# Gated embedding added to the residual by accumulating transfers instead of VectorE, in three of four column groups

## The chip, the core and the metric

The kernel runs on one core of one Trainium2 chip. The metric is the device time of one execution in microseconds (us), taken as the median over several runs of the same program. The profile is one further execution, recorded by the hardware profiler.

Five instruction streams matter here. TensorE (PE) multiplies matrices into the banks of PSUM. VectorE (DVE) and ScalarE (ACT) work on tiles of 128 rows. GpSimd (POOL) does almost no arithmetic in this kernel, but the transfers that add into their destination are issued from it. SyncE (SP) issues all the plain loads and stores of the part in question. Each engine takes its own instructions in a fixed order, and an instruction that waits for another engine or for a transfer holds back everything that stands behind it on its engine.

## The reference, cut to what matters

The block computes a residual stream `h` of 256 rows by 4096 columns (attention heads and a convolution module in parallel, projected and added to the input). The last stage, which the change touches, is this:

```python
gate = jax.nn.sigmoid(rms_norm(h, ple_norm_g[i]) @ w_ple_gate[i] + b_ple_gate[i])
h = h + gate * (p[i] @ w_ple[i])
return rms_norm(h, final_g)
```

`w_ple_gate` is 4096 x 4096 and `w_ple` is 256 x 4096, all in float32. The final norm needs, for each row, the sum of the squares of the new `h` over all 4096 columns before any column can be scaled and stored.

## The kernel before

**Products.** Every matrix product is done on high and low parts of its operands: ACT rounds a weight tile to a short format (`wh`, line 204), DVE subtracts that from the tile (`wl`, line 205), and PE adds three products (high by high, low by high, high by low). `mixed_product` computes a pair of 512-column blocks (1024 columns) for both halves of 128 rows. It walks over 16 pairs of weight row blocks. Half of the pairs in the last stage are done with seven block products instead of eight (a form of Strassen's method, marked `*` in the order strings): for these DVE also makes sums of weights (`ua`, `ub`, lines 518, 519, 531, 532), ACT and DVE split these sums (`uh`, `ul`), and four more PSUM banks, `P1`, `P5`, `P6` and `P7`, collect the helper products. The eight PSUM banks are thus used up: four hold the main sums `acc`, and four (the pool `ps_tmp`) hold the helpers. A plain pair is 24 matmuls, a pair of seven is 21.

**The last stage.** `gated_pair` (from line 1236 on) does one group of 1024 columns; it is called for three groups (`c0` = 0, 2, 4, here called G1, G2, G3), and the fourth group, G4, is written out behind it. At a group's end the product `p @ w_ple` of its columns is put into the four `ps_tmp` banks as `pacc`. Then four quarters follow (two blocks of columns by two halves of rows): DVE finishes the gate's argument (line 1266), ACT takes the sigmoid (line 1267), and four things are left for later: the multiplication of the gate with `pacc` (`z<-acc,z`, which I call the multiply), the addition to the residual (`hc<-hc,z`, the add), the sum of squares on ACT (line 610, the square), and the multiplication with the final norm's weight (`hc<-hc,row`, the weighting).

**What sets the order.** The deque `later` holds the work that is left over. `fill(4)` takes four entries from it after each pair of the next group, and so mixes the left work with the splitting of the next group's weights. The first pair of G2, G3 and G4 is plain (pair 1), the second is one of seven (pair `0*`), so the four `ps_tmp` banks must have been emptied by the multiplies before that second pair's helper products can begin. A scheduler then orders all instructions of each engine by their place in the program and by when it expects their inputs; only what is pinned keeps its place. Work therefore moves on all engines where the entries of `later` change.

Of the kernel before, what the change touches and what calls it, by code (L numbers as in the profile page):

```python
# [13 lines left out]
ALU = mybir.AluOpType  # L14
# [11 lines left out]
def hybrid_block(  # L26
# [23 lines left out]
    nc = tc.nc  # L50
# [129 lines left out]
    later = deque()  # L180
# [62 lines left out]
    def product(w, col, lhs, kblocks, pool=None, tag="acc", fills=2):  # L243

        acc = [
            (pool or ps_acc).tile([P, NB], F32, tag=tag, name=f"acc{h}") for h in range(NH)
        ]
        for k0 in range(0, kblocks, KC):
            kc = min(KC, kblocks - k0)
            wh, wl = weight_parts(w, col, k0, kc)  # L250
            for k in range(kc):
                for h in range(NH):
                    accumulate(acc[h], h, lhs, k0 + k, wh, wl, k, kblocks)
            fill(fills)
        return acc
# [313 lines left out]
    tt, stt = nc.vector.tensor_tensor, nc.vector.scalar_tensor_tensor  # L569
    QUARTERS = ((0, 0), (1, 0), (0, 1), (1, 1))  # L570

    def helper_sums(helper, z):


        nc.scalar.copy(z[1][0], helper["P1"])
        tt(z[1][0], helper["P6"], z[1][0], ALU.add)
        tt(z[0][1], helper["P5"], z[1][0], ALU.add)
        tt(z[1][0], helper["P7"], z[1][0], ALU.add)
        tt(z[1][1], helper["P5"], z[1][0], ALU.add)

    def sum_tiles(*homes):

        homes = homes or (dict(tag="stage"),) * 2
        t = [spool.tile([P, NH, NB], F32, name="z", **kw) for kw in homes]
        return t, [[t[j][:, h] for j in range(2)] for h in range(NH)]
# [481 lines left out]
    def broadcast_row(src, n0, n, **kw):  # L1067

        kw = kw or dict(tag="row", bufs=3)
        t = spool.tile([P, n], F32, name="row", **kw)  # L1070
        nc.sync.dma_start(
            t, bass.AP(tensor=src.tensor, offset=src.offset + n0, ap=[[0, P], [1, n]])
        )
        return t
# [122 lines left out]
    for c0 in range(0, D // NB, 2):  # L1197
        for j in range(2):
            hc = act.tile([P, NH, NB], F32, tag="act", name="hc")
# [20 lines left out]
        for h, j in QUARTERS:  # L1220
            hc = hs[c0 + j][:, h, :]
# [10 lines left out]
    ssq_f = cpool.tile([P, NH, n_f + 2], F32, name="ssq_f")  # L1232
    nc.vector.memset(ssq_f[:, :, :1], EPS)
    square_f = partial(square_sum, scale=D ** -0.5)

    def gated_pair(c0, order, ahead):

        z, rows, fgs = [], [], []

        def on_begin():  # L1240
            rows.extend(broadcast_row(b_ple_gate, (c0 + j) * NB, NB) for j in range(2))

        def on_helpers(helper):
            z.extend(sum_tiles()[1])
            stt(z[0][0], helper["P1"], r_h[:, :1], rows[0], ALU.mult, ALU.add)
            helper_sums(helper, z)
            for h, j in QUARTERS[1:]:
                zz = z[h][j]
                stt(
                    zz, zz, r_h[:, h : h + 1], rows[j],  # L1250
                    ALU.mult, ALU.subtract if j else ALU.add,
                )
            fgs.extend(broadcast_row(final_g, (c0 + j) * NB, NB) for j in range(2))

        acc = mixed_product(
            w_ple_gate[0], c0 * NB, hT, hS, order, on_helpers, ahead=ahead, fills=(4,),
            on_begin=on_begin,
        )
        pacc = [
            product(w_ple[0], (c0 + j) * NB, pT, PLE // P, pool=ps_tmp, tag="tmp", fills=0)  # L1260
            for j in range(2)
        ]
        todo = []
        for h, j in QUARTERS:
            gt, hc = z[h][j], hs[c0 + j][:, h, :]
            stt(gt, acc[h][j], r_h[:, h : h + 1], gt, ALU.mult, ALU.subtract if j else ALU.add)
            nc.scalar.activation(gt, gt, AF.Sigmoid)
            later.append(partial(tt, gt, pacc[j][h], gt, ALU.mult))
            todo.append(partial(tt, hc, hc, gt, ALU.add))
            todo.append(partial(square_f, ssq_f[:, h, 1 + c0 + j : 2 + c0 + j], hc))  # L1270
            todo.append(partial(tt, hc, hc, fgs[j], ALU.mult))
        later.extend(todo)

    for c0 in range(0, n_f - 2, 2):
        gated_pair(c0, dense if c0 else late, None if c0 else h_ahead)


    c0 = n_f - 2
# [9 lines left out]
    rows, fgs = [], []  # L1288
# [90 lines left out]
    squares = []  # L1379
# [45 lines left out]
```

## Time and profile before

| quantity | value |
|---|---|
| median of 3 runs | 2024.87 us |
| the 3 runs | 2024.87, 2024.77, 4118.48 us |
| profiled execution, device time | 2025.85 us |
| its span in the profile | 2024.1 us |
| mean granted PE clock | 0.998 |
| PE busy | 2006.7 us (99%) |
| DVE busy | 1926.9 us (95%) |
| ACT busy | 1257.1 us (62%) |
| POOL busy | 65.3 us (3%) |
| POOL transfers in the last stage | none (last one issued at 1615.2 us) |

The one run of 4118.48 us is twice the others and says nothing on the kernel; the other two agree. The profiled execution's own time stands 1.75 us above its span and 0.98 us above the median. In the trace's time, G1 ends and G2 begins at about 1745.6 us, G3 begins at 1833.3 us, G4 at 1921.2 us, and the span ends at 2024.1 us. "Busy" means that an instruction was being executed; waiting for a semaphore is not busy time.

### The profile page before, as it was taken

What the parts mean: (1) busy time and instruction counts of PE and PEld (TensorE: products, weight loads), DVE (VectorE), ACT (ScalarE), POOL (GpSimd) and SP (SyncE); (2) the same over time, 40 slices, a digit from 0 to 9 for tenths busy, and PEclk for the clock granted to TensorE, in tenths of its full rate; (3) what the DMA queues carried; (4) which work ended last, traced back from release to release, by engine and by line L of the source; (5) the groups of instructions that cost most, each with busy time, mean ns of one, the idle gap of its engine ahead of it and who ended that gap; (6) DMA issues with size and microseconds to landing.
All of it is one profiled execution on the core that took longest, in us unless ns stands there. A gap on an engine that the chain in (4) does not pass through costs nothing.

```text
span 2024.1 us, 26329 instructions
## 1 busy us (share of the span) xinstructions
PE 2006.7 (99%) x9043; PEld 1648.0 (81%) x9043; DVE 1926.9 (95%) x2771; ACT 1257.1 (62%) x1634; POOL 65.3 (3%) x71
## 2 busy tenths in 40 slices
PE   9999999999999999999999999999999999999997
PEld 7888888878888888788888888887888888888876
DVE  7999999899999999888999999999999999999998
ACT  7655555665666556776566676765766766656565
POOL 0000000000000000000000000000000000000000
PEclk9999999999999999999999999999999999999999
DMA  8788878679668877556677786876767766666765
GB/s 290 225 233 241 249 221 250 178 220 257 200 198 257 255 206 235 164 176 205 202 239 215 225 244 209 240 239 204 236 215 230 234 200 200 211 218 206 232 207 180
DMA packets 174193, 447.72 MB, mean 221 GB/s; under 512 B 14302, under 2 KB 17518, under 8 KB 174058
## 3 DMA queue, kind: packets, MB, share of 16 engines
q1 hardware_dynamic: 161952, 417.93, 63.8%
q0 software_dynamic: 11456, 27.27, 7.9%
q8 instruction: 71, 1.16, 0.2%
q10 hardware_dynamic: 650, 0.84, 0.1%
q14 instruction: 64, 0.52, 0.1%
HBM read 441.78 MB, written 4.19 MB: 220 GB/s over the span
## 4 chain that ended last, share of the span: by engine, by line
PE 89%; DVE 6%; issue 2%; DMA 1%; ACT 1%; POOLq 0%; POOL 0%; ACTq 0%; DVEq 0%; SPq 0%
PE acc L420 68%; PE acc_P L420 17%; DVE wl L205 2%; DMA wt<-in_w_in_dram 1%; PE tmp_ps L170 1%; DVE cv L787 1%; PE acc L237 1%; DVE ul L205 1%; PE tmp_ps L959 0%; PE tmp_ps L943 0%; PE tmp_ps L977 0%; ACT uh L204 0%; DVE cv L868 0%; ACT wh L204 0%; PE tmp_ps L982 0%
## 5 line engine op out<-in xcount | busy, mean ns | idle before, releaser
L420 PE MATMUL acc<-wh,big_t 128*128 128x512 f32 x4028 | 1240.3, 391 | 0.9 <-ACT big_t L156 0.4
L204 ACT CAST wh<-wt 128x1024 fp32r<-128x1024 f32 (+1 forms) x716 | 684.3, 965 | 493.8 <-PE acc L420 351.7
L420 PEld LDWEIGHTS acc<-wh,big_t 128*128 128x128 f32 x4028 | 753.3, 188 | 157.1 <-issue 1.3
L205 DVE TENSOR_TENSOR wl<-wt,wh 128x1024 fp32r<-128x1024 f32 (+1 forms) x716 | 788.8, 1113 | 33.0 <-ACT wh L204 27.5
L420 PE MATMUL acc<-wl,big_t 128*128 128x512 f32 x1958 | 756.4, 392 | 0.3 <-DVE wl L205 0.2
L420 PEld LDWEIGHTS acc<-wl,big_t 128*128 128x128 f32 x1958 | 367.2, 188 | 78.1 <-DVE wl L205 2.7
L204 ACT CAST uh<-ua 128x1024 fp32r<-128x1024 f32 x187 | 196.6, 1051 | 103.0 <-DVE ua L519 51.7
L205 DVE TENSOR_TENSOR ul<-ua,uh 128x1024 fp32r<-128x1024 f32 x187 | 228.1, 1220 | 6.9 <-ACT uh L204 4.2
L787 DVE SCALAR_TENSOR_TENSOR cv<-uT,dw,cv 128x255 f32<-128x255 f32 (+23 forms) x480 | 203.6, 463 | 1.1
L420 PE MATMUL acc_P<-uh,big_t 128*128 128x512 f32 x570 | 174.6, 391 | 0.1
L204 ACT CAST uh<-ub 128x1024 fp32r<-128x1024 f32 x99 | 104.2, 1053 | 47.9 <-DVE ub L532 39.2
L420 PEld LDWEIGHTS acc_P<-uh,big_t 128*128 128x128 f32 x570 | 106.0, 188 | 24.5 <-ACT uh L204 3.3
L205 DVE TENSOR_TENSOR ul<-ub,uh 128x1024 fp32r<-128x1024 f32 x99 | 120.8, 1220 | 0.8 <-ACT uh L204 0.5
L420 PE MATMUL acc_P<-ul,big_t 128*128 128x512 f32 x285 | 109.7, 392 | 0.2 <-DVE ul L205 0.2
L420 PE MATMUL acc<-uh,big_t 128*128 128x512 f32 x286 | 88.6, 390 | 0.0
L420 PE MATMUL acc_P<-wh,big_t 128*128 128x512 f32 x286 | 88.3, 389 | 0.0
L518 DVE TENSOR_TENSOR ua<-wt 128x512 f32<-128x512 f32 x112 | 76.9, 686 | 10.0 <-DMA wt<-in_w_in_dram 6.2
L519 DVE TENSOR_TENSOR ua<-wt 128x512 f32<-128x512 f32 x112 | 76.8, 686 | 2.7 <-DMA wt<-in_w_in_dram 1.7
L420 PE MATMUL acc_P<-uh,comb_t 128*128 128x512 f32 x228 | 70.3, 391 | 0.3 <-ACT uh L204 0.2
L532 DVE TENSOR_TENSOR ub<-ub,wt 128x512 f32<-128x512 f32 x99 | 68.1, 688 | 1.4
L531 DVE TENSOR_TENSOR ub<-ua,wt 128x512 f32<-128x512 f32 x99 | 67.8, 685 | 0.0
L420 PEld LDWEIGHTS acc_P<-ul,big_t 128*128 128x128 f32 x285 | 53.3, 188 | 13.9 <-DVE ul L205 3.0
(254 smaller groups left out, 1631.0 us busy)
## 6 DMA issues: line engine op xcount, KB each, us to landing
wt<-in_w_in_dram SPq DMA_DIRECT2D x416, 512.0 KB, 4.7
wt<-in_w_out_dram SPq DMA_DIRECT2D x128, 512.0 KB, 4.5
wt<-in_w_ple_gate_dram SPq DMA_DIRECT2D x128, 512.0 KB, 4.2
wt<-in_w_pw_dram SPq DMA_DIRECT2D x32, 512.0 KB, 4.9
ua<-in_w_in_dram SPq DMA_DIRECT2D x31, 512.0 KB, 4.3
ua<-in_w_in_dram POOLq DMA_DIRECT2D x31, 512.0 KB, 8.8
wt<-in_w_in_dram SPq DMA_DIRECT2D x31, 256.0 KB, 2.8
low<-in_w_in_dram POOLq DMA_DIRECT2D x12, 512.0 KB, 8.2
```

What stands on the lines that cost most here:

```text
L170: nc.tensor.transpose(pt[:, i * T + h * P : i * T + (h + 1) * P], src[:, h, b] if len(src.shape) == 4 else src[:, h, b * P : (b + 1) * P], ...
L204: nc.scalar.copy(wh[:, :kc, :], wt[:, :kc, :]),
L205: nc.vector.tensor_tensor(wl[:, :kc, :], wt[:, :kc, :], wh[:, :kc, :].bitcast(F32), ALU.subtract),
L237: nc.tensor.matmul(acc, a, b[:, k, :], start=kb == 0 and kind == 0, stop=kb == kblocks - 1 and kind == 2,)
L420: nc.tensor.matmul(banks[name], a, b, start=name not in begun, stop=final and ends[name] == n and kind == 2 and not (left and name in "P2 ...
L518: plus(ua[:, 0], w0[:, 0], w0[:, 1])
L519: plus(ua[:, 1], w0[:, 1], w1[:, 1])
L531: plus(ub[:, 0], ua[:, 0], w1[:, 1])
L532: plus(ub[:, 1], ub[:, 0], w1[:, 0])
L787: nc.vector.scalar_tensor_tensor(cv[:, i, PAD - k :], uT[:, i, : T + k - PAD], dw[:, b, k : k + 1], cv[:, i, PAD - k :], ALU.mult, ALU.add,)
```

## The change

Two edits in `gated_pair`, so in the three groups G1 to G3; G4 is as it was.

```diff
-        todo = []
+        squares, weights = [], []
         for h, j in QUARTERS:
             gt, hc = z[h][j], hs[c0 + j][:, h, :]
             stt(gt, acc[h][j], r_h[:, h : h + 1], gt, ALU.mult, ALU.subtract if j else ALU.add)
             nc.scalar.activation(gt, gt, AF.Sigmoid)
             later.append(partial(tt, gt, pacc[j][h], gt, ALU.mult))
-            todo.append(partial(tt, hc, hc, gt, ALU.add))
-            todo.append(partial(square_f, ssq_f[:, h, 1 + c0 + j : 2 + c0 + j], hc))
-            todo.append(partial(tt, hc, hc, fgs[j], ALU.mult))
-        later.extend(todo)
+            later.append(partial(nc.gpsimd.dma_start, hc, gt, accum_op=ALU.add))
+            squares.append(partial(square_f, ssq_f[:, h, 1 + c0 + j : 2 + c0 + j], hc))
+            weights.append(partial(tt, hc, hc, fgs[j], ALU.mult))
+        later.extend(squares + weights)
```

The add of each quarter, a DVE instruction on 128 x 512 float32, becomes a transfer issued from POOL that reads `gt` in SBUF and adds it into `hc` in SBUF: 256 KB each, 12 in all. The 16 entries of a group also stand in another sequence. Before: four multiplies, then add, square, weighting of each quarter. Now: multiply and transfer of each quarter in turn, then four squares, then four weightings. With four entries taken after each pair, two multiplies and two transfers are now taken behind the first pair, the other two of each behind the second (`0*`), the squares behind the third and the weightings behind the fourth.

The scheduler makes of this the following. First ACT at the start of G2, with the sigmoids of G1 behind us. `uh_15712`, `wh_15716` and `uh_15723` are the high parts for pair `0*`; `hc_11728` and `hc_11730` are the residual blocks of G1, `junk` the unused output of a square. A semaphore whose name begins with `DMASW` belongs to a transfer issued from POOL. Before:

```order
L204 CAST wh_15677<-wt_15659 128x1024 [waits DMAHW0_49,PE_49,Activation_49]
L204 CAST wh_15705<-wt_15697 128x512 [waits DMAHW1_49,PE_49,Activation_49]
L204 CAST uh_15712<-ua_15709 128x1024 [waits DVE_49]
L204 CAST wh_15716<-wt_15699 128x1024 [waits DMAHW4_49,PE_49,Activation_49]
L204 CAST wh_15761<-wt_15757 128x1024 [waits DMAHW5_49,DVE_49,PE_49]
L204 CAST wh_15777<-wt_15759 128x1024 [waits DMAHW6_49,DVE_49,PE_49]
L204 CAST uh_15723<-ub_15720 128x1024 [waits DVE_49]
L610 ACTIVATE junk_15753,ssq_f_14773<-hc_11728 128x512
L204 CAST wh_15803<-wt_15799 128x512 [waits DMAHW7_49,PE_49,Activation_49]
L610 ACTIVATE junk_15793,ssq_f_14773<-hc_11728 128x512 [waits DVE_49,Activation_49]
```

And ACT at the same place now:

```order
L204 CAST uh_15712<-ua_15709 128x1024 [waits DVE_49]
L610 ACTIVATE junk_15792,ssq_f_14773<-hc_11728 128x512 [waits DMASW4_49]
L610 ACTIVATE junk_15794,ssq_f_14773<-hc_11728 128x512 [waits DMASW5_49,Activation_49]
L204 CAST wh_15716<-wt_15699 128x1024 [waits DMAHW4_49,PE_49]
L204 CAST uh_15723<-ub_15720 128x1024 [waits DVE_49]
L204 CAST wh_15760<-wt_15756 128x1024 [waits DMAHW5_49,PE_49]
L204 CAST wh_15776<-wt_15758 128x1024 [waits DMAHW6_49,PE_49]
L610 ACTIVATE junk_15796,ssq_f_14773<-hc_11730 128x512 [waits DMASW6_49,Activation_49]
L204 CAST wh_15804<-wt_15800 128x512 [waits DMAHW7_49,DVE_49,PE_49]
L610 ACTIVATE junk_15798,ssq_f_14773<-hc_11730 128x512 [waits DMASW7_49,Activation_49]
L204 CAST uh_15811<-ua_15808 128x1024 [waits DVE_49]
```

All four squares moved up, each in front of a cast for the next matmuls, and each now waits for a transfer. At the starts of G3 and G4 ACT's order is nearly the same, except that one square, not two, stands ahead of the cast that corresponds to `wh_15716`.

Then DVE at the same place. `z_15518` and `z_15519` hold the gates, `acc1_15606`, `acc0_15625` and `acc1_15626` are banks with `pacc`. Before:

```order
L184 TENSOR_TENSOR z_15518<-acc1_15606,z_15518 128x512 [waits PE_49,Activation_49]
L519 TENSOR_TENSOR ua_15709<-wt_15697,wt_15699 128x512 [waits DMAHW4_49]
L184 TENSOR_TENSOR z_15519<-acc0_15625,z_15519 128x512 [waits PE_49,Activation_49]
L205 TENSOR_TENSOR wl_15678<-wt_15659,wh_15677 128x1024 [waits DMAHW0_49,DVE_49,Activation_49]
L184 TENSOR_TENSOR z_15519<-acc1_15626,z_15519 128x512 [waits PE_49]
L205 TENSOR_TENSOR wl_15706<-wt_15697,wh_15705 128x512 [waits DVE_49,Activation_49]
L205 TENSOR_TENSOR ul_15713<-ua_15709,uh_15712 128x1024 [waits Activation_49]
L205 TENSOR_TENSOR wl_15717<-wt_15699,wh_15716 128x1024 [waits PE_49,Activation_49]
L531 TENSOR_TENSOR ub_15720<-ua_15709,wt_15699 128x512
L184 TENSOR_TENSOR hc_11728<-hc_11728,z_15518 128x512
```

And DVE now:

```order
L184 TENSOR_TENSOR z_15518<-acc1_15606,z_15518 128x512 [waits PE_49,Activation_49]
L519 TENSOR_TENSOR ua_15709<-wt_15697,wt_15699 128x512 [waits DMAHW4_49]
L531 TENSOR_TENSOR ub_15720<-ua_15709,wt_15699 128x512 [waits DVE_49]
L205 TENSOR_TENSOR wl_15678<-wt_15659,wh_15677 128x1024 [waits DMAHW0_49,Activation_49]
L205 TENSOR_TENSOR wl_15706<-wt_15697,wh_15705 128x512 [waits DVE_49,PE_49,Activation_49]
L205 TENSOR_TENSOR ul_15713<-ua_15709,uh_15712 128x1024 [waits Activation_49]
L532 TENSOR_TENSOR ub_15720<-ub_15720,wt_15699 128x512 [waits DVE_49]
L205 TENSOR_TENSOR wl_15717<-wt_15699,wh_15716 128x1024 [waits PE_49,Activation_49]
L184 TENSOR_TENSOR z_15519<-acc0_15625,z_15519 128x512
L205 TENSOR_TENSOR ul_15724<-ub_15720,uh_15723 128x1024 [waits Activation_49]
L184 TENSOR_TENSOR z_15519<-acc1_15626,z_15519 128x512
```

The third multiply (of `acc0_15625`) moved behind `wl_15717`, which needs the cast `wh_15716`, and the fourth behind `ul_15724`; the adds are gone. Further on in DVE's order the four weightings now stand close together behind the second pair of seven (`2*`), at the sums `ub_15819` and ahead of `ul_15823`.

Last, PE at the helper products of pair `0*`, as they stand now:

```order
L420 MATMUL acc_P7_15703<-uh_15712,big_t_14665 128x512 [waits DVE_49]
L420 MATMUL acc_P7_15703<-uh_15712,big_t_14665 128x512
L420 MATMUL acc_P7_15703<-ul_15713,big_t_14665 128x512
L420 MATMUL acc00_15653<-wh_15716,big_t_14664 128x512 [waits Activation_49]
L420 MATMUL acc00_15653<-wh_15716,big_t_14664 128x512
L420 MATMUL acc00_15653<-wl_15717,big_t_14664 128x512
```

Before, the first of these rows had no wait of its own; now it waits for DVE, namely for the third multiply to empty the bank that `P7` takes over.

## The prediction

> **What bounds the kernel now.** I read the page first (busy time by engine), then the stretches of the last stage, then the chain of waits in order of time.
>
> ```profile
> span 2024.1 us, 26329 instructions
> PE 2006.7 (99%) x9043; PEld 1648.0 (81%) x9043; DVE 1926.9 (95%) x2771; ACT 1257.1 (62%) x1634; POOL 65.3 (3%) x71
> PE 89%; DVE 6%; issue 2%; DMA 1%; ACT 1%; POOLq 0%; POOL 0%; ACTq 0%; DVEq 0%; SPq 0%
> ```
>
> PE is the bound, with DVE right behind it. For the last stage the next view gives, by stretch, the length, then the busy time of each engine, the clock, and the transfers' share and rate.
>
> ```profile
> core 0: us, PE busy (x) PEld busy (x) DVE busy (x) ACT busy (x) POOL busy (x), PEclk, DMA share, GB/s
> 1746.00:1784.00 38.00, 37.95 (x167) 30.70 (x166) 37.97 (x47) 23.00 (x31) 0.00 (x0) 1.00 0.62 201
> 1784.00:1834.00 50.00, 50.00 (x221) 41.06 (x220) 49.30 (x60) 29.47 (x33) 0.00 (x0) 1.00 0.71 228
> 1834.00:1872.00 38.00, 38.00 (x166) 30.72 (x166) 37.85 (x48) 23.09 (x31) 0.00 (x0) 1.00 0.62 192
> ```
>
> Both engines are full: at each group's start (first and third row) DVE is busy for practically all of it, while ACT has 15 us to spare in 38 and POOL does nothing. How much PE could gain is read from the chain, whose rows give start and length:
>
> ```profile
> 1740.13 5.44 PE acc L237 x24
> ...
> 1827.88 5.44 PE acc L237 x24
> ...
> 1915.73 5.44 PE acc L237 x24
> ```
>
> These are the same 24 matmuls at the ends of G1, G2 and G3. One takes 5.44 / 24 = 0.2267 us of PE's time. A group has 8 x 24 + 8 x 21 + 24 = 384, so 87.05 us, and the groups follow each other after 87.75 and 87.85. PE waits 0.7 and 0.8 us in a group; with about 1 us in G4, 2.5 us is the most that any relief of DVE at these three places can bring.
>
> **The adds leave DVE.**
>
> ```profile
> L184 DVE TENSOR_TENSOR hc<-hc,z 128x512 f32<-128x512 f32 x12 | 8.1, 685 | 0.0
> L610 ACT ACTIVATE junk<-hc 128x512 bf16<-128x512 f32 (+1 forms) x33 | 20.3, 615 | 5.0 <-DVE hc L1332 2.3 <-DVE hc L1222 1.3 <-DVE end L1342 1.0
> ```
>
> Twelve adds of 0.60 us (start to start in the rows below) are 7.2 us of DVE, 2.4 a group. The gain is not 7.2 but at most the 2.5 us above, since PE is the next limit at once. The squares and the weightings keep their number and price; only their places change.
>
> **The transfers' own price.** Twelve issues occupy an idle POOL. The nearest rows: the accumulating loads of 512 KB (issue on POOL, time to landing), the two queues, a plain store of 256 KB out of the same tile, and the plain weight load.
>
> ```profile
> q1 hardware_dynamic: 161952, 417.93, 63.8%
> q0 software_dynamic: 11456, 27.27, 7.9%
> wt<-in_w_ple_gate_dram SPq DMA_DIRECT2D x128, 512.0 KB, 4.2
> out_dram<-hc SPq DMA_DIRECT2D x12, 256.0 KB, 2.4
> ...
> L524 POOL DMA_DIRECT2D low<-in_w_out_dram x6: 859/860/872, 1445.6 to 1615.2; - x6
> ...
> DMA to landing us min/median/max: 5.8/8.3/10.0
> ```
>
> The last row is for all 21 loads of that kind. In q0 all the traffic is accumulating: 0.079 x 2024.1 us for 27.27 MB, so 3.07 us of 16 engines for 512 KB, against 1.62 us in q1. Half the bytes take 1.5 us off the median of 8.3 if a transfer has the engines alone, and 3.1 if it shares them evenly: 6.8 or 5.2 us. Off the fastest, 5.8, it leaves 4.3. I call the time from issue to landing T and take 5.3, close to the lower value, because a source in SBUF rather than memory should be no slower, and these transfers share the engines (share 0.62). The ends: at least 2.4 + 0.87 = 3.3 us (the plain store plus POOL's issue), at most 8.4 (as slow as twice the bytes). The load on the engines, 12 x 1.5 = 18 us in 264, raises a share of about 0.65 by 0.07; I cost it at nothing, since weight loads that land in 4.2 us are issued ahead into five tiles. If that cover is gone, DVE's sums `ua` are late first.
>
> [...]
>
> **What now stands behind the transfers.** This is the term that decides. At the start of G2, DVE, ACT and PE before (start, length):
>
> ```profile
> 1743.34 1.28 DVE L184 TENSOR_TENSOR z<-acc,z 128x512 f32<-128x512 f32 x2
> ...
> 1747.47 0.68 DVE L205 TENSOR_TENSOR wl<-wt,wh 128x512 fp32r<-128x512 f32 x1
> 1748.07 1.22 DVE L205 TENSOR_TENSOR ul<-ua,uh 128x1024 fp32r<-128x1024 f32 x1
> 1749.23 1.23 DVE L205 TENSOR_TENSOR wl<-wt,wh 128x1024 fp32r<-128x1024 f32 x1
> 1750.38 0.69 DVE L531 TENSOR_TENSOR ub<-ua,wt 128x512 f32<-128x512 f32 x1
> ```
>
> ```profile
> 1745.95 1.05 ACT L204 CAST uh<-ua 128x1024 fp32r<-128x1024 f32 x1
> 1748.15 1.06 ACT L204 CAST wh<-wt 128x1024 fp32r<-128x1024 f32 x1 [1.14 <-issue]
> ...
> 1753.68 0.63 ACT L610 ACTIVATE junk<-hc 128x512 bf16<-128x512 f32 x1
> 1754.21 0.19 ACT L610 ACTIVATION_READ_ACCUMULATOR junk<-hc 128x1 f32 x1
> 1754.30 0.61 ACT L204 CAST wh<-wt 128x512 fp32r<-128x512 f32 x1
> ```
>
> ```profile
> 1752.21 0.61 PE L420 MATMUL acc_P<-uh,big_t 128*128 128x512 f32 x2
> ...
> 1766.04 0.39 PE L420 MATMUL acc_P<-ul,big_t 128*128 128x512 f32 x1
> ```
>
> The steps from start to start: DVE 0.60 us for 512 columns and 1.14 to 1.16 for 1024, ACT 0.62 for a square.
>
> - The first multiply ends at 1744.0, so the first transfer lands at 1744.1 + 5.3 = 1749.4, the second, behind POOL's 0.87 us of issue, at about 1750.4. ACT is done with `uh` at 1747.0 and stands before the first square. The second square ends at 1751.1. Only then comes the cast of `wh` that began at 1748.15.
> - Behind it: cast 1.05, subtraction 1.14, third multiply 0.60, plus hand-over: 1754.0. PE wants the bank that this multiply frees at 1752.21: a wait of 1.8 us.
> - The third transfer, issued at 1754.0, lands at 1759.3. Behind it stand, in series, the third square 0.62, a cast of 512 columns 0.56, its `wl` 0.60, three sums 1.8, a weighting 0.60, `ul` 1.14, `wl` 1.14, the last sum 0.60, three weightings 1.8, `wl` 1.14 and `ul` 1.14. That is 11.1 us, so this `ul` is ready at about 1770.6. The fourth transfer's square is ready before this chain needs it.
> - Before, PE took that `ul` at 1766.04, with three more matmuls (0.7 us) already behind it. G2 is late by 4.6 + 0.7 = 5.3 us.
>
> G3 is milder, since one square, not two, stands ahead of the cast, and that cast came late before too:
>
> ```profile
> 1830.79 0.69 DVE L184 TENSOR_TENSOR z<-acc,z 128x512 f32<-128x512 f32 x1
> ...
> 1835.85 1.06 ACT L204 CAST wh<-wt 128x1024 fp32r<-128x1024 f32 x1 [2.05 <-PE acc L420]
> ...
> 1854.31 0.39 PE L420 MATMUL acc_P<-ul,big_t 128*128 128x512 f32 x1
> ```
>
> First multiply done at 1831.4, landing 1836.8, square, cast from 1837.45 (not 1835.85), third multiply done at 1840.3, landing 1845.7, and 11.1 us later 1856.8 instead of 1854.31: 2.5 us, and 0.4 for the order of matmuls, 2.9. G4 has the same order: 2.9.
>
> **The sum.** 5.3 + 2.9 + 2.9 = 11.1 us. Of the 2.5 us that PE waits now, the part that lies further on in the groups, which a lighter DVE ends, I put at 1.5. Net 9.6 us on the profiled execution's 2025.85: 2035.4; that execution stands 1.0 above the median, so 2034.4 against 2024.87. I say 2035, slower by 0.5%. Since two landings stand in series at each of three places, each us of T is worth 6 us: at T = 3.7 the sum is nothing, at 8.4 it is 9.6 + 6 x 3.1 = 28.
>
> **The rivals.**
> - *The transfers are hidden* (chance 0.22). If T is at most 3.7, the squares find their blocks ready, DVE's 2.4 us a group remain as a gain, and PE's waits of 2.5 us go: 2022.4 to 2025. For it speaks the plain store (2.4 us), against it the fastest accumulating load, 5.8.
> - *The transfers are slower, or one waits for the other* (0.22). At T = 8.4 the time is 2053. If the second of a pair starts when the first has landed, the second square of G2 comes 4.3 us later and the chains of G3 and G4 some 2.5: about 2044. For it speaks the slowest load (10.0); nowhere before do two such transfers stand back to back, so the trace excludes neither.
> - *More than 2% slower* (0.03) would need 40 us, so T near 10, or weight loads that come late throughout.
> - The forecast itself, T from 3.7 to 6.5, so 2025 to 2042, has 0.53.
>
> The range from 2022 to 2053 takes in both ends of T (2022.4 and 2053), and so the forecast, the hidden case and most of the slow one; about 1 in 10 is left out. A change of 2%, 40 us, is about what a measurement of this kernel can tell from none. The ceiling of 2.5 us makes faster by that much as good as impossible (0.01), slower 0.03, within 0.96.
>
> **What would show it.** Right: squares of line 610 that idle ACT for a POOL transfer, two to three us at each group's start; PE waiting on DVE before `acc_P` products; DVE idle near 1749 and 1758, busy again after. Groups of some 92, 90 and 90 us. Wrong: landings below 4 us, or squares whose blocks had long landed; then the groups stay at 87 us. If DVE's own instructions became longer beside the transfers, none of these sums holds.

## The result and the profile after

| quantity | before | after |
|---|---|---|
| median | 2024.82 us (4 runs) | 2050.41 us (4 runs, 2047.13 to 2052.18) |
| ratio to before | | 1.0118, 95% interval 1.0105 to 1.0131 |
| span of the profiled execution | 2024.1 us | 2050.4 us |
| PE busy | 2006.7 us | 2015.0 us |
| span less PE busy | 17.4 us | 35.4 us |

The kernel is slower by 25.6 us where 10 were forecast. (One of before's four runs, 4118.48 us, is the same outlier as in the table above and is left out of the ratio.) The two medians alone give 1.0126, inside the interval. The kernel before had medians of 2025.95, 2026.48 and 2027.07 us where the runs below were timed, so the 25.6 us are known to about 2. First the page of the kernel after: busy time by engine and the queue that carries POOL's transfers.

```profile
PE 2015.0 (98%) x9043; PEld 1653.1 (81%) x9043; DVE 1922.5 (94%) x2759; ACT 1258.1 (61%) x1634; POOL 75.8 (4%) x83
...
q0 software_dynamic: 13184, 30.41, 8.7%
```

Twelve DVE instructions are gone (2771 to 2759) and DVE is 4.4 us lighter. But PE, with the same 9043 matmuls, is busy 8.3 us longer, and idle 18.0 us longer. Together they are the 26.3 us by which the span grew. So there are two effects to explain, waits and longer matmuls. Nearly all of both lies in G2 to G4: from the first of the 24 matmuls at G1's end to the same matmul of G4, PE was idle for 0.2 us of 257.6 before and for 16.6 of 282.3 after, and busy for 257.3 and 265.7.

The waits stand at the groups' starts. ACT at the start of G2 after the change (start, length, and in brackets the idle time ahead and what ended it):

```profile
1750.03 0.63 ACT L610 ACTIVATE junk<-hc 128x512 bf16<-128x512 f32 x1 [1.96 <-DMA hc<-z]
...
1752.52 0.63 ACT L610 ACTIVATE junk<-hc 128x512 bf16<-128x512 f32 x1 [1.77 <-DMA hc<-z]
...
1753.15 1.03 ACT L204 CAST wh<-wt 128x1024 fp32r<-128x1024 f32 x1
...
1760.75 0.63 ACT L610 ACTIVATE junk<-hc 128x512 bf16<-128x512 f32 x1 [3.73 <-DMA hc<-z]
...
1764.57 0.63 ACT L610 ACTIVATE junk<-hc 128x512 bf16<-128x512 f32 x1 [2.59 <-DMA hc<-z]
...
1765.20 1.04 ACT L204 CAST uh<-ua 128x1024 fp32r<-128x1024 f32 x1
```

All four squares idle ACT until a transfer lands, and behind the second and the fourth stands a cast that the next matmuls need. The waits view of the last stage sums such rows (total us, times, longest):

```profile
ACT junk L610 <- DMA hc<-z: 29.0, 12, 3.7
DVE wl L205 <- ACT wh L204: 17.0, 16, 3.6
PE acc_P L420 <- DVE z L184: 7.5, 3, 2.7
PE acc_P L420 <- DVE ul L205: 6.7, 6, 1.8
```

Before, the second of these lines read as follows, and PE had no wait long enough to be listed:

```profile
DVE wl L205 <- ACT wh L204: 1.1, 3, 0.5
```

This reads as a chain from top to bottom: ACT waits for all twelve transfers, DVE for ACT's casts, PE for DVE. The chain of waits in order of time names the transfers that set the end, two for each group's start:

```profile
1746.30 6.13 DMA hc<-z
...
1758.42 6.07 DMA hc<-z
...
1843.85 6.94 DMA hc<-z
...
1855.02 6.03 DMA hc<-z
...
1940.93 6.42 DMA hc<-z
...
1951.58 5.95 DMA hc<-z
```

They are the second and the fourth of their group's four. In G3 these two left POOL at

```profile
1843.85 0.88 POOL L184 DMA_DIRECT2D hc<-z  x1 [1.12 <-DVE ua L519]
...
1855.02 0.86 POOL L184 DMA_DIRECT2D hc<-z  x1 [1.81 <-PE acc L420]
```

Last the longer matmuls. Stretches of 4 us; behind the busy times of the five engines stand the granted clock of PE and the transfers' share and rate:

```profile
core 0: us, PE busy (x) PEld busy (x) DVE busy (x) ACT busy (x) POOL busy (x), PEclk, DMA share, GB/s
1774.00:1778.00 4.00, 4.00 (x13) 3.14 (x12) 3.97 (x7) 1.04 (x1) 0.00 (x0) 0.61 0.85 273
1778.00:1782.00 4.00, 4.00 (x19) 3.26 (x18) 3.39 (x4) 2.91 (x4) 0.00 (x0) 0.96 0.53 148
1870.00:1874.00 4.00, 4.00 (x11) 3.14 (x12) 3.97 (x6) 1.05 (x1) 0.00 (x0) 0.57 0.93 284
1946.00:1950.00 4.00, 1.51 (x6) 1.17 (x6) 2.71 (x3) 3.16 (x6) 0.87 (x1) 0.87 0.47 133
1950.00:1954.00 4.00, 4.00 (x14) 3.24 (x13) 3.21 (x4) 1.93 (x5) 0.86 (x1) 0.70 0.73 167
1966.00:1970.00 4.00, 3.60 (x10) 2.89 (x11) 3.96 (x7) 0.68 (x1) 0.00 (x0) 0.57 0.96 272
```

In the third row PE is busy for all 4 us but does 11 matmuls, where the second has 19. The clock is well below 1.00 in four places, each just behind a wait of PE; before the change every such stretch stood at 1.00.

### The profile page after: what moved, and what is told of

Read it like the earlier page. It is cut to its first block, busy times and chain, and to the rows that moved or that the text cites. A ratio compares the mean times of both kernels' runs of the same rounds, so it can differ in the third digit from the quotient of the medians.

```text
span 2050.4 us, 26341 instructions
## 1 busy us (share of the span) xinstructions
PE 2015.0 (98%) x9043; PEld 1653.1 (81%) x9043; DVE 1922.5 (94%) x2759; ACT 1258.1 (61%) x1634; POOL 75.8 (4%) x83
```

## The experiments

All are the changed kernel with one edit. "Us" below is the median less the median of the kernel before on the same chip; after itself is +25.6.

**1. The new order without transfers.**

```diff
-            later.append(partial(nc.gpsimd.dma_start, hc, gt, accum_op=ALU.add))
+            later.append(partial(tt, hc, hc, gt, ALU.add))
```

> The entries of a group stand in the changed kernel's sequence, but each add is again a DVE instruction; no transfer is issued from POOL in the last stage. Theory A (the cost is that ACT and, behind it, DVE and PE wait for the transfers' landings): nothing lands here, so 2023 to 2028 us. Rival B (the sequence itself costs: the third and fourth multiply come too late for the helper banks, and squares stand ahead of casts): 2040 us or more.

Measured: 2025.23 us, ratio 0.9996 (0.9987 to 1.0006). The written sequence costs nothing by itself. The scheduler's order is not quite that of the change, though: in G2 the third multiply stands ahead of its `wl` (1748.19 and 1748.79) and the fourth ahead of its `ul`, where the change has both behind. So this run clears the sequence as it is written; the order on the engines is tested by runs 2 and 3.

**2. The same transfers, squares later.** The transfers stay; squares and weightings are taken two pairs later, and each square is tied behind the casts made before it.

```diff
-            squares.append(partial(square_f, ssq_f[:, h, 1 + c0 + j : 2 + c0 + j], hc))
+            square = partial(square_f, ssq_f[:, h, 1 + c0 + j : 2 + c0 + j], hc)
+            squares.append(partial(behind_casts, square))
...
-        later.extend(squares + weights)
+        idle_turns = [lambda: None] * 8
+        later.extend(idle_turns + squares + weights)
```

Here `behind_casts` makes the square inside `queued_behind(list(recent))`.

> The changed kernel with the twelve transfers where they were; the squares and weightings are taken two pairs later, and each square is tied behind the casts of the pair at which it is taken. Theory A: the blocks have landed when ACT reaches the squares, so PE's waits go and 2021 to 2027 us remain. Rival B (multiplies late): these have not moved back, so 2035 us or more. Rival C (the transfers' load on the transfer engines or on POOL and DVE costs by itself): the load is unchanged, so 2040 to 2050 us.

Measured: 2024.69 us, ratio 0.9992 (0.9983 to 1.0001). The transfer view of this kernel (count, size, median us from issue to landing) shows that the transfers were as slow as ever:

```profile
hc<-z POOLq DMA_DIRECT2D x12, 256.0 KB, 6.2
```

No square waits for one of them, and PE's busy time is 2003.3 us. On DVE the third and fourth multiply stand in G2 behind `wl` and `ul`, as in the change, so multiplies that come late are not the cause either. The load of twelve accumulating transfers costs nothing that can be measured; all 25.6 us come from what stands behind the landings.

**3. A plain copy in place of the accumulation.** The order on every engine is that of the change.

```diff
-            later.append(partial(nc.gpsimd.dma_start, hc, gt, accum_op=ALU.add))
+            later.append(partial(nc.gpsimd.dma_start, hc, gt))
```

> The changed kernel in which the twelve transfers from POOL copy the gated embedding over the residual block instead of adding it (the residual is left out of these three groups); the order on every engine is the same. Theory A: only the time to landing changes, from a median of 6.0 us to perhaps 3.5 to 4.5; at 6 us of time for each us to landing and without most of the slow PE clock, 2030 to 2042 us. Rival B (order): unchanged, 2048 to 2052 us. Rival C (load): half of the engine time goes, about 2038.

Measured: 2032.26 us, +6.3, ratio 1.0028 (1.0018 to 1.0038). The transfer view and the waits view:

```profile
hc<-z POOLq DMA_DIRECT2D x12, 256.0 KB, 3.2
```

```profile
ACT junk L610 <- DMA hc<-z: 13.1, 10, 2.9
```

By the medians, the same bytes land in little more than half the time without the accumulation, and three quarters of the loss go. PE's busy time is 2005.4 us: no halved clock here.

**4. Half the bytes.** The accumulation covers 256 of the 512 columns; the order on every engine is again that of the change.

```diff
-            later.append(partial(nc.gpsimd.dma_start, hc, gt, accum_op=ALU.add))
+            later.append(partial(nc.gpsimd.dma_start, hc[:, : NB // 2], gt[:, : NB // 2], accum_op=ALU.add))
```

> The changed kernel in which each of the twelve accumulating transfers adds only the first 256 of 512 columns (the other columns' embedding is left out); the order on every engine is the same. Theory A: the time to landing falls by the share that goes with bytes, 0.8 to 1.5 us of 6.0, so 5 to 9 us less than the changed kernel and about 2 us less from the slow clock: 2039 to 2045 us. Rival B: 2048 to 2052 us. Rival C: half the excess, 2037.

Measured: 2042.24 us, +16.3, ratio 1.0081 (1.0066 to 1.0096); span 2040.4, PE busy 2010.4. The transfer view, and the first and last of the six transfers in the chain of waits:

```profile
hc<-z POOLq DMA_DIRECT2D x12, 128.0 KB, 5.2
```

```profile
1745.55 3.93 DMA hc<-z
...
1943.45 5.25 DMA hc<-z
```

Halving the bytes takes only 0.8 us off the median landing. The six landings in its chain sum to 31.8 us (mean 5.3), those of after to 37.5 (mean 6.26). PE's idle time is 30.0 us here and 35.4 there. So 5.7 us of landing make 5.4 of idle time: the chain runs through six landings, about one for one. (In G4 of this run the chain names the first transfer in place of the second.) By chance this is the kernel with just the T that the prediction took.

**5 and 6. Which transfer of a pair?** Half the bytes for the first and third transfer alone, then for the second and fourth alone.

```diff
-            later.append(partial(nc.gpsimd.dma_start, hc, gt, accum_op=ALU.add))
+            part = slice(0, NB // 2 if h == 0 else NB)
+            later.append(partial(nc.gpsimd.dma_start, hc[:, part], gt[:, part], accum_op=ALU.add))
```

(The other has `h == 1`.)

> The changed kernel in which the first and third transfer of each group add only 256 of 512 columns (the rest of their embedding is left out); the second and fourth are whole, and the order on every engine is the same. Theory A1 (the chain runs over the second and fourth transfer, since their landings come last, 1.3 and 2.6 us after the work behind the third is ready): little is won, 2044 to 2051 us. Theory A2 (as the prediction had it: the chain runs over the first and third): most of what halving all four won is won, 2041 to 2044 us.

> The changed kernel in which the second and fourth transfer of each group add only 256 of 512 columns (the rest of their embedding is left out); the first and third are whole. Theory A1: 2040 to 2045 us. Theory A2: 2046 to 2051 us.

Measured: first and third 2048.45 us, +22.0, ratio 1.0109 (1.0095 to 1.0122); second and fourth 2043.66 us, +17.2, ratio 1.0088 (1.0073 to 1.0104). Lightening the second and fourth alone gives nearly all that lightening the four gives (+16.3). The intervals touch only at 1.0095 and 1.0104, so the difference of 4.8 us is likely rather than certain, and it agrees with the chain above, which names these transfers. PE's idle time from G1's end to G4's, which leaves the longer matmuls out, says it more clearly: 16.6 us after, 16.2 with the first and third halved, 11.4 with the second and fourth, 12.0 with all four. In G3 and G4 it was the fourth transfer alone that gained: it landed in 2.99 and 3.01 us in run 6 (6.03 and 5.95 after), while the second, with half its bytes, took 6.90 and 6.62 (6.94 and 6.42 after).

**7. Filling PE's second wait.** To see whether the halved clock comes of PE's waits, seven matmuls by zeros stand ahead of the helper product that waits for sums in the second pair of seven, in G2 to G4.

```diff
+            if keep_warm and n == 3:
+                for _ in range(7):
+                    pin(nc.tensor.matmul(banks["P6"], zeros, w1h[:, 0], start=False, stop=False))
             add("P6", s_of(2), (ubh[:, 0], ubl[:, 0]), n, True)
```

> The changed kernel with seven more matmuls, of zeros, ahead of the P6 products of the second pair of seven in G2, G3 and G4 (1.6 us of PE's time each), where PE waits 0.23 and 1.8 us. Theory H (PE's clock falls to half for some microseconds because of the idle time ahead): the matmuls fill the wait, the clock stays up behind it, and 3 to 5 us are won, 2045 to 2047 us. Rival (the slow stretch has another cause, such as the transfers): no change, or up to 2 us more, 2049 to 2053 us.

Measured: 2051.44 us, +25.0, ratio 1.0124 (1.0111 to 1.0138): no gain, so the expected time failed. But the clock moved. Stretches of G2 and G3 behind the first and the second wait:

```profile
1754.00:1758.00 4.00, 3.02 (x7) 2.45 (x8) 4.00 (x6) 1.90 (x3) 1.57 (x2) 0.62 0.61 166
1774.00:1778.00 4.00, 4.00 (x20) 3.27 (x19) 3.91 (x7) 2.39 (x3) 0.00 (x0) 1.00 0.94 291
1850.00:1854.00 4.00, 3.05 (x7) 2.48 (x8) 3.41 (x5) 3.34 (x5) 0.93 (x2) 0.57 0.64 165
1870.00:1874.00 4.00, 4.00 (x19) 3.29 (x18) 3.97 (x7) 1.62 (x2) 0.00 (x0) 1.00 0.83 268
```

Behind the filled wait (second and fourth row) it now stands at 1.00, where after had 0.61 and 0.57; behind the unfilled first wait (2.96 and 2.66 us here) it is halved instead, where after had none in G2 and G3.

**8. Multiplies first.** The best version that the findings suggest: four multiplies, then four transfers, and the squares as in 2.

```diff
-            later.append(partial(nc.gpsimd.dma_start, hc, gt, accum_op=ALU.add))
+            adds.append(partial(nc.gpsimd.dma_start, hc, gt, accum_op=ALU.add))
...
+        later.extend(adds + idle_turns + squares + weights)
```

> All four multiplies of a group first, then its four transfers, then the squares, two pairs later and tied behind the casts, then the weightings. Nothing that feeds PE stands behind a landing, and the banks of pacc are freed as early as in the kernel before; DVE has 2.4 us a group less to do. Theory A: at most the 2.5 us that PE waits in these groups are won, so 2021 to 2025 us where the kernel before has 2025. If the transfers' load costs by itself: 2026 to 2030.

Measured: 2024.22 us, ratio 0.9991 (0.9983 to 1.0000). It undoes the whole loss. That it beats the kernel before is not shown: the interval ends at 1.0000, and its other end is 3.4 us of gain.

**9. Filling both waits.** Twelve more matmuls by zeros, ahead of the helper product that waits for the third multiply.

```diff
+            if keep_warm and n == 1:
+                for _ in range(12):
+                    pin(nc.tensor.matmul(banks["P2"], zeros, w0h[:, 0], start=False, stop=False))
             add("P7", s_of(0), (uah[:, 1], ual[:, 1]), n, True)
```

> The run e7_fill_wait filled only the second long wait of a group; the halved clock then stood behind the first wait instead. Here both are filled: 12 matmuls by zeros (2.7 us at full clock) ahead of the helper product that waits for the third multiply in G2, G3 and G4, and 7 (1.6 us) ahead of the one that waits for the sums of the second pair of seven. They add nothing to the result. The scheduler moves some casts and sums at these places, so waits may shift. H (PE's waits bring the halved clock): the clock stays at 1.00 in every 4 us stretch of the three groups, PE's busy time is that of the kernels without long waits, 2005.4, plus 57 x 0.227 = 12.9, so 2018, and PE's idle time falls from 35 us by about 12. Time: the 8.3 us of slow matmuls go and the fill covers idle time, so about 2042 (2040 to 2045). R (the halved clock has another cause, such as the transfers or the load on ACT and DVE): some stretches stay near 0.6 to 0.8, PE is busy for 2023 or more, and the time stays at 2050.

Measured: 2057.33 us, +30.3, ratio 1.0150 (1.0133 to 1.0167): both expected times failed. With the longer PE queue the scheduler also put other casts first, and the second wait now stands ahead of an earlier product that nothing fills. That wait, and a stretch behind it, in G3:

```profile
1869.78 0.50 PE L420 MATMUL acc<-wl,big_t 128*128 128x512 f32 x1 [1.82 <-DVE wl L205]
```

```profile
1870.00:1874.00 4.00, 4.00 (x12) 3.15 (x12) 4.00 (x6) 1.04 (x1) 0.00 (x0) 0.61 0.78 231
```

The halved clock followed the wait to its new place. Filling does not help here, since the waits stay, or move, and the fill has its own price.

## Why the prediction was off

**Right: the mechanism.** The squares wait for the landings, hold back the casts behind them, and PE stands before `acc_P` products. Run 2 shows it from the other side: same transfers, no square behind them, no loss. Also right were the transfers' load, costed at nothing (run 2; weight loads still land in 4.2 us), and the ceiling on the gain: the two best versions, 2 and 8, stand at -1.3 and -2.3 us with intervals that reach zero. The slope of 6 us for each us of T is borne out in PE's idle time by run 4. The measured 1.2% stands clear of noise, so the 2% that I named as the least that can be told from none was too careful.

**Wrong: the sum.** It was 9.6 us; the spans give 26.3. Run 4 had T = 5.3 by its chain, as the prediction took it, and so separates the terms:

| term | us |
|---|---|
| predicted | 9.6 |
| same T, more idle time: 30.0 - 17.4 = 12.6 instead of 9.6 | +3.0 |
| landings of 6.26 instead of 5.3: idle time 35.4 - 30.0 | +5.4 |
| same matmuls, longer: 2015.0 - 2006.7 | +8.3 |
| sum | 26.3 |

Each row compares single executions. Kernels without these waits (before, runs 1, 2 and 8) idle PE for 17.4 to 19.8 us, so the smallest row, 3.0, is uncertain by some 2 us; within G2 to G4 alone the idle time of run 4 grew by 11.8 us. (G2's arithmetic also has a slip of 0.2 us: 1759.3 + 11.1 is 1770.4.)

*The first term* fails at "The fourth transfer's square is ready before this chain needs it" and at "G3 is milder". I hung the second wait of each group on the third transfer, and the first wait of G3 and G4 on the first transfer. G3 shows what it hangs on instead. ACT and then DVE there, after the change:

```profile
1850.87 0.63 ACT L610 ACTIVATE junk<-hc 128x512 bf16<-128x512 f32 x1 [1.02 <-DMA hc<-z]
...
1851.49 1.03 ACT L204 CAST uh<-ub 128x1024 fp32r<-128x1024 f32 x1
...
1861.13 0.63 ACT L610 ACTIVATE junk<-hc 128x512 bf16<-128x512 f32 x1 [3.61 <-DMA hc<-z]
...
1861.76 1.03 ACT L204 CAST uh<-ua 128x1024 fp32r<-128x1024 f32 x1
```

```profile
1852.56 1.23 DVE L205 TENSOR_TENSOR ul<-ub,uh 128x1024 fp32r<-128x1024 f32 x1 [0.85 <-ACT uh L204]
1853.70 0.68 DVE L184 TENSOR_TENSOR z<-acc,z 128x512 f32<-128x512 f32 x1
```

The second square holds back the cast `uh`, that holds back `ul`, and behind `ul` stands the fourth multiply. So the fourth transfer leaves late (1855.02), and its square at 1861.13 holds back ACT for 3.61 us and with it the next cast `uh`, on which the sums for the second pair of seven depend. The third transfer landed at 1856.20, after only 3.85 us; by my 11.1 us behind it this `ul` would have been ready at 1867.3, and PE took it at 1869.92. In all three groups the fourth multiply stands behind a `ul`, and a cast behind the fourth square, whatever stands ahead of their first cast. How late PE then is, its timeline tells: the first of the 24 matmuls at the ends of G1 and G2, and the product with the `ul` that it waited for. After the change:

```profile
1741.04 0.62 PE L237 MATMUL acc<-wh,big_t 128*128 128x512 f32 x2
...
1773.36 0.50 PE L420 MATMUL acc_P<-ul,big_t 128*128 128x512 f32 x1 [1.81 <-DVE ul L205]
...
1837.04 0.61 PE L237 MATMUL acc<-wh,big_t 128*128 128x512 f32 x2
...
1869.92 0.50 PE L420 MATMUL acc_P<-ul,big_t 128*128 128x512 f32 x1 [1.79 <-DVE ul L205]
```

And the same two matmuls before (the timeline sets their start 0.16 us ahead of the chain's rows that the prediction shows):

```profile
1739.97 0.61 PE L237 MATMUL acc<-wh,big_t 128*128 128x512 f32 x2
...
1827.72 0.62 PE L237 MATMUL acc<-wh,big_t 128*128 128x512 f32 x2
```

From the one to the other it is now 32.32 us in G2 and 32.88 in G3. Before it was 26.07 (1766.04 - 1739.97) and 26.59 (1854.31 - 1827.72). Both groups' `ul` is late by 6.3 us, where I had 4.6 and 2.5: G3 is no milder. With the slower clock behind it G2 takes 96.00 us (1837.04 - 1741.04) instead of 87.75, where I had said 92.

*The second term* is a size. I took T = 5.3 from loads of twice the bytes less the time of half of them; the six that matter took 5.95 to 6.94. That a source in SBUF is no slower than memory, one of my two reasons for 5.3, is not shown: no run accumulates the same bytes from both. Run 4 shows why halving was no good guide: from 128 to 256 KB the median rises by only 0.8 us, and T hangs on the transfer's place in its group as much as on its size (table at the end). The plain store of 2.4 us was no guide either; the plain copy of run 3 landed in 3.2 us by its median.

*The third term* was not in the sum at all. I costed the clock at nothing, since it stood at 1.00 in every row of before. A wait of PE was priced at its length, but each wait behind which the clock fell cost up to 1.71 us more (below). I never asked what the waits that I had forecast would do to the clock. How many of them it falls behind is partly luck: four of six in this execution.

**The rivals.** That the transfers are hidden is excluded by the waits view, though runs 2 and 8 reach it by another order. The slower transfers with T near 8.4 did not happen (longest 6.94); the time came near that rival's 2053 for other reasons. That one transfer waits for the other is half true: the second was issued 0.60 us behind the first in G2 and 1.99 and 1.97 us behind it in G3 and G4, and landed 2.4 to 2.6 us behind it in all three. In G2 that is some 1.8 us of delay, where the rival had 4.3.

Open is why an issue of POOL comes some 0.6 us after its multiply is done (0.66, 0.64 and 0.64 us for the second, third and fourth of G3); no run tried it.

## What to carry to other kernels

Moving work from a full engine to a transfer replaces an instruction by a landing time, and whatever reads the result must then be placed behind other ready work on its own in-order engine: here the same transfers cost 25.6 us with the squares early and nothing with them two pairs later. When a forecast contains waits of the engine that is the bound, follow every transfer of the group to its reader, the last one too, and bound the price of each wait by its length and by its length plus what a lower clock behind it adds (1.71 us in after, 3.4 us once in run 6).

## What the runs showed of the hardware

**PE's clock fell to half behind waits of 1.78 to 2.96 us.** Matmuls that begin 0.227 us apart otherwise began 0.43 us apart, as in G2 of after:

```profile
1775.67 1.05 PE L420 MATMUL acc<-wh,big_t 128*128 128x512 f32 x2
1776.52 0.63 PE L420 MATMUL acc<-wl,big_t 128*128 128x512 f32 x1
1776.95 1.05 PE L420 MATMUL acc<-wh,big_t 128*128 128x512 f32 x2
```

In the six rows by stretch shown first, the loss is 4 us times what is missing of 1.00: 4 x (0.39 + 0.04) = 1.72 us in G2, 4 x 0.43 = 1.72 in G3, 4 x (0.13 + 0.30) = 1.72 and 4 x 0.43 = 1.72 in G4. Finer stretches show why it is always the same: each time the clock stood at 0.50 for 3.41 us, so half of that, 1.71 us, was lost (the fall of run 6 lasted 6.9 us). Four make 6.8 of the 8.3 us; the rest I put down to matmuls that start right behind a wait (0.50 us in place of 0.39), an estimate that I did not sum up. G4 has two such places, G2 and G3 one each.

Over the groups G2 to G4 of all the kernels, the clock fell only at a wait of PE of 1.78 us or more, and at 13 of the 25 such waits; kernels whose waits stayed below that (before, runs 1, 2, 3 and 8; at most 1.75 us, in run 3) stood at 1.00 in every stretch of 4 us, though runs 2 and 8 had the same transfers. Together with runs 7 and 9, where the place moved with the unfilled wait, this ties it to the waits, though no run showed the time that it costs on its own.

The traces also show which waits were spared. In after the clock fell at 1774.90, 1870.47, 1948.98 and 1966.04 us. These places lie 95.57, 78.51 and 17.06 us apart, which is 28, 23 and 5 times 3.413 us, so in this execution the changes lie on a fixed grid of windows of that length. In runs 5, 7 and 9 the falls are likewise 23, 28, 29 and 29 windows apart, as closely as stretches of 4 us can tell (78.5, 95.6, 99.0 and 99.0 us). Cut along this grid, after has the following at the first wait of G2 (2.65 us, no fall) and at the second of G3 (1.79 us, a fall); the columns are those of the stretches shown first:

```profile
1751.00:1754.41 3.41, 2.44 (x11) 1.69 (x9) 0.20 (x1) 1.89 (x4) 0.00 (x0) 1.00 0.79 290
1754.41:1757.83 3.42, 1.74 (x8) 1.42 (x8) 3.42 (x5) 2.61 (x3) 0.87 (x1) 1.00 0.38 108
1867.05:1870.47 3.42, 1.63 (x6) 1.03 (x7) 3.42 (x4) 1.29 (x2) 0.00 (x0) 1.00 0.93 282
1870.47:1873.88 3.41, 3.41 (x9) 2.64 (x8) 3.38 (x6) 1.04 (x1) 0.00 (x0) 0.50 0.87 297
```

The longer wait is shared by two windows, which idle PE for 0.97 and 1.68 us; the shorter one lies within a single window, which idles it for 1.79, and the next window runs at half clock. So it is over G2 to G4 of the six kernels in which the clock fell (after, runs 4 to 7 and 9), each cut along its own grid and windows already at half clock left aside: behind each of the 12 windows with 1.79 us of idle time or more the clock fell, behind none with 1.62 or less, and of the five windows between behind one (1.64 us in after; not 1.68 and 1.77 there, 1.72 in run 5 and 1.75 in run 6). Every wait of 1.78 us or more that was spared had been cut by the grid, so that no window idled PE for 1.79 us or more.

**An accumulating transfer within SBUF was slow to land, and its place mattered as much as its size.** 256 KB took 6.0 us in after (median of 12, 3.9 to 6.9), 128 KB 5.2 in run 4 (3.2 to 6.2), and a plain copy of 256 KB 3.2 in run 3 (2.5 to 5.6). By place in the group, the medians of G2, G3 and G4 are, in us from issue to landing:

| transfer | after | plain copy (3) | all halved (4) | first and third halved (5) | second and fourth halved (6) |
|---|---|---|---|---|---|
| first | 5.9 | 4.4 | 5.9 | 5.6 | 6.1 |
| second | 6.4 | 5.0 | 6.1 | 7.0 | 6.6 |
| third | 3.9 | 3.1 | 3.2 | 3.2 | 3.9 |
| fourth | 6.0 | 2.5 | 5.3 | 6.2 | 3.0 |

At the same place the plain copy took 0.8 to 1.6 us less, and 3.5 less at the fourth. Half the bytes gained little at the first two places; at the fourth they landed in 5.3 us in one kernel and in 3.0 in another. The weight loads under way beside a transfer differ between these kernels; that they make the difference was not tested.
